# VectorE in program order for the last two expert units of layer 0, with the merge of read-back results moved

## The chip, the cores and the metric

The kernel is one program on one NeuronCore of a Trainium2 chip. A core has TensorE (PE, the matrix engine; PEld is its weight load), VectorE (DVE), ScalarE (ACT), GpSimd (POOL) and SyncE (SP, which here only issues transfers). The engines run independently and wait for one another through semaphores; each executes its own queue in order. Transfers go through 16 DMA engines. The metric is device microseconds of one execution; the median of three runs of the kernel before is 1012.01 us.

## The reference

The reference is a transformer backbone of two layers over 256 context and 256 latent tokens, width 1024. Each layer has a mixer (layer 0 a recurrent one, layer 1 attention) and a mixture of experts. This is the part that matters here, with `t` the 512 normalised tokens of layer 0:

```python
e_val, e_idx = lax.top_k(e_sel, TOP_K)            # two experts for each token
...
for e in range(N_EXPERTS):                        # 16 experts, hidden width 512
    he = jax.nn.silu(t @ w1[e]) * (t @ w3[e])
    out = out + comb[:, e:e + 1] * (he @ w2[e]).astype(F32)
...
xl = xl + g2l * hier_moe(hl2, ...)                # the residual, gated
```

Layer 1 begins with an RMS norm of that sum, and then the qkv projection.

## The kernel before, in words

The 16 experts of layer 0 are computed in 12 units (`NU`), each on at most 128 gathered rows. Units with `SEQ[e] >= BIG` serve two experts, 64 rows each, straight from the loaded weights (`raw`) in f32; the others split each weight half into a high and a low part (`whi` by ScalarE, `wlo` by VectorE) and take three matmuls for one product. In the loop over `e` from line 1825 a unit has these steps: first inner product (`hidden(e, 0, ...)`, issued one unit ahead), `sl` = silu of it, second inner product (`hidden(e, 1, 0)` and `hidden(e, 1, 1)`), `he` = product of both (line 1840), its transposes, `hh` and, for split units, the low part `hl` (line 1853), then the output product in two accumulators `py`. While unit `e` waits for `he`, the first inner product of unit `e + 1` is on PE.

The loop's last two units are positions 10 (split; `SEQ` 7) and 11 (two experts; `SEQ` 11). The results of positions 0 to 9 are scattered to a buffer `yd` in HBM. The results of the last two stay on chip: `yh` and `yl` are the high and low part of `py` times the routing weight, and `finish_moe` multiplies them by a one-hot matrix (`back`) to bring them back to token order.

At position 10 (`NU - N_LAST`) `get_parts` lets GpSimd read `yd` back: two transfers of 512 KB (`ya`, `yb`) for each of four tiles of 128 tokens, in the order `F_ORDER` = 2, 3, 0, 1. For tiles 0 and 1 both halves lie in a buffer named `pt`. `merge(t)` (line 1813) adds `ya` and `yb`, multiplies by the gate row and adds the sum to the residual `xres[t]`: four VectorE instructions, of which the multiplication is two. In `finish_moe` (line 1902) the products of the last two units are gated and added to `xres`; from it comes the norm of layer 1.

The order of instructions: without a pin a scheduler places an engine's instructions by priority and dependence as it estimates them. `pin(where)` reads the table `PIN` (line 61) and keeps the engines named there (p PE, a ScalarE, d VectorE, g GpSimd) in the order of the program text, until the next `pin`. `m0` before the loop pins PE alone; `fin` behind it has no entry, so nothing is pinned from there.

Weights come from one planned list by SyncE; a load is issued when its buffer comes free. Behind the weights of unit 11 (twelve loads of 1 MB, of which the last is the one called the twelfth) the list goes on with loads for layer 1 (`w_ada`, `w_qkv`). All computing instructions carry line 131 in the profile, since a helper issues them; they are told apart by tile names.

Of the kernel before, what the change touches and what calls it, by code (L numbers as in the profile page):

```python
# [27 lines left out]
NU = 12  # L28
# [29 lines left out]
N_ADA = 2  # L58
Q0 = (0, 0, 2, 2, 2, 2, 1, 1, 1, 1)
LT_ACT = 1  # L60
PIN = dict(pair='p', px='padg', re='da', tb='dag', m0='p', n1='pad', xa='pad')
AT_SUM = 1
N_SP0 = 2
N_OH = 1
# [38 lines left out]
F_ORDER = (2, 3, 0, 1)  # L103
# [35 lines left out]
def backbone(ctx, tc, I, out):  # L139
# [3 lines left out]
    def pin(where):  # L143
        names = PIN.get(where, "")
        for e, nm in ((act, "a"), (dve, "d"), (pool, "g"), (pe, "p"), (sp, "s")):
            e.on = nm in names
# [11 lines left out]
    def acc():  # L158
        return acc_p.tile([P, 512], F32, tag="acc", name="acc")

    def aux():
        return aux_p.tile([P, 512], F32, tag="aux", name="aux")
# [68 lines left out]
    def feed(key):  # L231
        state["fed"] = where[key]
        pump(state["fed"] + len(slots))
        return loaded.pop(key)

    def less_slots(pl):
        state["turn"] = sum(p is not pl for p, _ in slots[:state["turn"]])
        slots[:] = [x for x in slots if x[0] is not pl]
# [306 lines left out]
    def high_if(x):  # L545
        return tc.high_priority() if x else ExitStack()

    def mm3(ps, a, b, first, last):

        pe.matmul(ps, a[0], b[0], start=first, stop=False)  # L550
        pe.matmul(ps, a[0], b[1], start=False, stop=False)
        pe.matmul(ps, a[1], b[0], start=False, stop=last)
# [219 lines left out]
    def fetch_moe(l, d4, t, NT):  # L772
        ys = d4("ya"), d4("yb")
        for k, y in enumerate(ys):
            (sp if l else pool).dma_start(y, yd[l][(k * NT + t) * P:(k * NT + t + 1) * P, :])
        return ys
# [483 lines left out]
    def wide(name="w"):  # L1260
        if name in IN_B.split():
            return raw2_p.tile([P, 2048], F32, tag="raw", name=name).rearrange("p (m n) -> p m n", m=4)
        return wp.tile([P, 4, 512], F32, tag="w", name=name)
# [34 lines left out]
    xa, u = wide("xa"), wide("u")  # L1298
# [149 lines left out]
    for d in range(2):  # L1448
        seq = list(range(8)) if d == 0 else [3, 2, 1, 0, 7, 6, 5, 4]
        for ct in range(2):  # L1450
            n4 = 2 * d + ct
            dsb = [aux(), aux()]
            for c in seq[:-1]:
                pr, t = c % 2, c // 2
# [39 lines left out]
    for tpr in range(2):  # L1494
# [29 lines left out]
        for ti in range(2):  # L1524
            t = 2 * tpr + ti
# [123 lines left out]
    def d4(name):  # L1649
        return wk.tile([P, D], F32, tag="d4", name=name, bufs=N_D4)  # L1650
# [9 lines left out]
    def fetch_x(i):  # L1660
        if i < NU:
            if i < 2:
                xg = xgs[i] = xg01[:, i * D:(i + 1) * D]
            else:
                xg = xgs[i] = d4("xg")
            if 2 <= i < N_D4:
                pool.memset(xg, 0.0)
            gather(0, xg, ix[:, SEQ[i]:SEQ[i] + 1])
# [41 lines left out]
    def halves(ps, lhsT, raws, sl, first, last):  # L1710

        for o in range(2):
            c = slice(o * (P // 2), (o + 1) * (P // 2))
            pe.matmul(ps[c, :], lhsT[:, c], raws[o][:, sl], start=first, stop=last)
# [15 lines left out]
    def quarters(i, n, h):  # L1730
        ahead()
        for q in range(2):
            yield q, *split_of.pop(((i, n, h), q))
            state["done"] += 1
            ahead()

    def hidden(i, n, h):
        if h == 0:
            hs[i, n] = acc()
        xh, xl = xs[i]  # L1740
        if SEQ[i] >= BIG:
            raws = [feed((n, 0, i, o, h)) for o in range(2)]
            for kk in range(4):
                k = 4 * h + kk
                halves(hs[i, n], xh[:, k, :], raws, slice(kk * 512, (kk + 1) * 512), k == 0, k == KD - 1)
            return
        for q, wh, wl in quarters(i, n, h):
            for kk in range(2):
                k = 4 * h + 2 * q + kk
                mm3(hs[i, n], (xh[:, k, :], xl[:, k, :]), [x[:, kk * 512:(kk + 1) * 512] for x in (wh, wl)],  # L1750
                    k == 0, k == KD - 1)
# [51 lines left out]
    def get_parts():  # L1803

        state["cap"] = len(order)
        for t in F_ORDER:
            if t < N_PARTS:
                pt = parts_p.tile([P, 2048], F32, tag="raw", name="pt")
                parts[t] = fetch_moe(0, {"ya": pt[:, 0:D], "yb": pt[:, D:2 * D]}.get, t, 4)
            else:  # L1810
                parts[t] = fetch_moe(0, d4, t, 4)

    def merge(t):

        ya, yb = parts[t]
        dve.tensor_tensor(ya, ya, yb, op=ALU.add)
        for n in range(2):
            sl = slice(n * 512, (n + 1) * 512)
            dve.tensor_tensor(ya[:, sl], ya[:, sl], g2[int(t < 2)][n], op=ALU.mult)
        dve.tensor_tensor(xres[:, t, :], xres[:, t, :], ya, op=ALU.add)  # L1820
# [4 lines left out]
    for e in range(NU):  # L1825
        two = SEQ[e] >= BIG
        if AHEAD > 2:
            fetch_x(e + AHEAD)
        if e == NU - N_LAST:
            get_parts()  # L1830
        sl = wk.tile([P, 512], F32, tag="sl", name="sl")
        act.activation(sl, hs[e, 0], AF.Silu)
        hidden(e, 1, 0)
        if e == NU - 1:
            for t in F_ORDER[:2]:
                merge(t)
        hidden(e, 1, 1)
        he = wk.tile([P, 4, P], F32, tag="he", name="he")
        with high_if(HE):
            dve.tensor_tensor(he.rearrange("q k p -> q p k"), sl.rearrange("q (p k) -> q p k", k=4),  # L1840
                              hs[e, 1].rearrange("q (p k) -> q p k", k=4), op=ALU.mult)
        if e + 1 < NU:
            hidden(e + 1, 0, 0)
        ps = aux()
        for k in range(4):
            pe.transpose(ps[:, k * P:(k + 1) * P], he[:, k, :], ident)
        hh = wk.tile([P, 512], F32 if two else F32R, tag="hh", name="hf" if two else "hh")
        if not two:
            hl = wk.tile([P, 512], F32R, tag="hl", name="hl")
        with high_if(HE):  # L1850
            act.activation(hh, ps, AF.Copy)
            if not two:
                dve.tensor_tensor(hl, ps, hh.bitcast(F32), op=ALU.subtract)
        if e + 1 < NU:
            hidden(e + 1, 0, 1)
        if e == NU - 1:
            for t in F_ORDER[2:]:
                merge(t)
        py = [acc(), acc()]
        for h in range(2):  # L1860
            if two:
                raws = [feed((2, 0, e, o, h)) for o in range(2)]
                for n in range(2):
                    for kk in range(2):
                        k = 2 * h + kk
                        halves(py[n], hh[:, k * P:(k + 1) * P], raws,
                               slice(kk * D + n * 512, kk * D + (n + 1) * 512), k == 0, k == 3)
            else:
                for q, wh, wl in quarters(e, 2, h):
                    k = 2 * h + q  # L1870
                    ks = slice(k * P, (k + 1) * P)
                    for n in range(2):
                        ws = slice(n * 512, (n + 1) * 512)
                        mm3(py[n], (hh[:, ks], hl[:, ks]), (wh[:, ws], wl[:, ws]), k == 0, k == 3)
            if h == 0 and e + 2 < NU:
                prep_x(e + 2)
        if e == NU - LESS:
            less_slots(parts_p)
        if e == 1:
            last_ow = d4("ow")  # L1880
            for n in range(N_LAST):
                last_tokens(NU - 1 - n)
            A1B1 = ada_cols(1)
        if e == 2:
            for n in range(N_LAST):
                turn_last(NU - 1 - n)
        if e == 4:
            g2 = [rows_pe(rowt, i, 2, mod[0], 2) for i in range(2)]
        if e >= NU - N_LAST:
            yh, yl = last_y[e] = [wk.tile([P, D], F32R, tag="d4", name="yl", bufs=N_D4) for _ in range(2)]  # L1890
            for n in range(2):
                sl = slice(n * 512, (n + 1) * 512)
                act.activation(yh[:, sl], py[n], AF.Copy, scale=wgt[:, SEQ[e]:SEQ[e] + 1])
                dve.scalar_tensor_tensor(yl[:, sl], py[n], wgt[:, SEQ[e]:SEQ[e] + 1], yh[:, sl].bitcast(F32),
                                         op0=ALU.mult, op1=ALU.subtract)
        else:
            y = d4("y")
            for n in range(2):
                act.activation(y[:, n * 512:(n + 1) * 512], py[n], AF.Copy, scale=wgt[:, SEQ[e]:SEQ[e] + 1])
            scatter(0, ix[:, NU + SEQ[e]:NU + SEQ[e] + 1], y)  # L1900
# [76 lines left out]
    px = ExitStack()  # L1977
# [533 lines left out]
```

## Time and profile before

| | |
|---|---|
| timed runs | 1014.98, 1012.01, 1007.88 us (median 1012.01) |
| the profiled execution | 1008.28 us, its span 1006.6 us |
| PE busy | 905.5 us (90% of the span) |
| VectorE busy | 540.6 us (54%) |
| ScalarE busy | 396.5 us (39%) |
| GpSimd busy | 130.3 us (13%) |
| read from HBM | 294.76 MB |
| memory rate over the span | 305 GB/s |

The profile is one execution. In the timeline a row is: start and duration in us, engine, line, operation, written tile `<-` read tiles, count of instructions merged in the row, and in brackets the idle time of the engine before it and what ended that. Matmuls are pipelined, so a row's duration is longer than the step from one start to the next. In the queue's tables q1 holds SyncE's transfers and q0 GpSimd's.

### The profile page before, as it was taken

Reading aid. Unit: us, or ns where it says so; the run is one execution under the profiler, and the core shown is the slowest. Engines: PE = TensorE matmul, PEld = TensorE weight load, DVE = VectorE, ACT = ScalarE, POOL = GpSimd, SP = SyncE. Lnnn points to the kernel's source line nnn. Section 1 sums busy time; section 2 is a strip of 40 time slices with the busy share of each in tenths; the row PEclk is TensorE's granted clock in tenths of the full one; section 3 lists DMA queues with packets and bytes.
Section 4 is the critical chain, followed back from the end, with each engine's and each line's share of the span. In section 5 each row is a group of like instructions: output and inputs, shape, how many; then the busy total and the mean of one; then the engine's idle time right before and its main releaser. Section 6 shows DMA issues by size and latency. Waiting matters only on the chain. (4 is left out here: it accounts for less than half of the span.)

```text
span 1006.6 us, 12582 instructions
## 1 busy us (share of the span) xinstructions
PE 905.5 (90%) x4565; PEld 535.6 (53%) x4565; DVE 540.6 (54%) x1040; ACT 396.5 (39%) x686; POOL 130.3 (13%) x142
## 2 busy tenths in 40 slices
PE   5999989999964989999999377999996999999997
PEld 3556456667744647457568133764574444443442
DVE  5495777458684656428468357787656111111112
ACT  3465472234322637347468104543644221121210
POOL 1011520133302112100001100133001000000000
PEclk9999999999995999999999788999998899999999
DMA  9957353488453899999998957655758699999994
GB/s 311 385 177 271 126 209 124 170 299 299 147 185 137 309 418 419 419 420 411 415 420 347 402 211 291 257 208 211 271 200 334 231 416 418 415 417 414 417 413 159
DMA packets 63166, 304.56 MB, mean 303 GB/s; under 512 B 8579, under 2 KB 17667, under 8 KB 35057
## 3 DMA queue, kind: packets, MB, share of 16 engines
q1 hardware_dynamic: 55216, 284.56, 72.5%
q0 software_dynamic: 5120, 14.06, 3.6%
q10 hardware_dynamic: 2752, 4.98, 1.3%
q8 instruction: 40, 0.66, 0.3%
q14 instruction: 38, 0.30, 0.1%
HBM read 294.76 MB, written 12.58 MB: 305 GB/s over the span
## 5 line engine op out<-in xcount | busy, mean ns | idle before, releaser
L131 DVE TENSOR_TENSOR wlo<-raw,whi 128x1024 fp32r<-128x1024 f32 x144 | 174.3, 1231 | 64.7 <-ACT whi L131 62.4
L131 ACT ACTIVATE whi<-raw 128x1024 fp32r<-128x1024 f32 x140 | 145.6, 1057 | 99.5 <-PE acc L131 86.3
L131 PE MATMUL aux<-raw,x 128*64 128x512 f32 x488 | 116.3, 597 | 1.1 <-ACT x L131 0.7
L131 PEld LDWEIGHTS aux<-raw,x 128*64 128x64 f32 x488 | 34.4, 137 | 62.3 <-issue 58.4
L131 PE MATMUL acc<-raw,xf 128*64 128x512 f32 x256 | 61.9, 598 | 2.9 <-DMA raw<-in_w_dram 2.9
L131 PE MATMUL aux<-raw,sl 128*64 128x512 f32 x240 | 57.0, 594 | 0.7 <-ACT sl L131 0.7
L131 PE MATMUL ada<-raw,cT 128*32 128x512 f32 x320 | 56.4, 613 | 0.1
L131 PE MATMUL acc<-whi,xh 128*128 128x512 f32 x128 | 51.9, 405 | 0.0
L131 PE MATMUL acc<-wlo,xh 128*128 128x512 f32 x128 | 50.1, 391 | 0.8 <-DVE wlo L131 0.8
L131 PE MATMUL acc<-whi,xl 128*128 128x512 f32 x128 | 50.1, 391 | 0.0
L131 PE MATMUL acc<-whi,hl 128*128 128x512 f32 x64 | 26.4, 413 | 20.5 <-DVE hl L131 20.5
L131 DVE SCALAR_TENSOR_TENSOR aux<-aux,ws,mod 128x512 f32<-128x512 f32 x8 | 6.1, 758 | 71.6 <-PE aux L131 71.6
L131 PE MATMUL acc<-whi,h 128*128 128x512 f32 x128 | 43.1, 410 | 0.0
L131 PE MATMUL acc<-hhi,whi 128*128 128x512 f32 x96 | 37.0, 415 | 3.3 <-ACT hhi L131 2.8
L131 PEld LDWEIGHTS acc<-raw,xf 128*64 128x64 f32 x256 | 19.2, 136 | 38.6 <-issue 30.0
L131 DVE TENSOR_TENSOR he<-sl,aux 128x512 f32<-128x512 f32 x8 | 8.5, 1057 | 56.2 <-PE aux L131 56.2
L131 PE MATMUL acc<-raw,hf 128*64 128x512 f32 x128 | 34.5, 600 | 4.3 <-DMA raw<-in_w_dram 4.3
L131 POOL DMA_INDIRECT yd<-y,ix x10 | 11.9, 1192 | 198.5 <-ACT y L131 182.2
L131 PEld LDWEIGHTS aux<-raw,sl 128*64 128x64 f32 x240 | 17.8, 137 | 35.8 <-issue 33.7
L131 PE MATMUL acc<-hlo,whi 128*128 128x512 f32 x96 | 35.9, 409 | 0.0
L131 PE MATMUL acc<-hhi,wlo 128*128 128x512 f32 x96 | 35.0, 400 | 0.0
L131 ACT ACTIVATE x<-gat,B,A 128x256 f32<-128x256 f32 x26 | 13.3, 561 | 41.6 <-PE gat L131 40.8
(438 smaller groups left out, 1823.9 us busy)
## 6 DMA issues: line engine op xcount, KB each, us to landing
raw<-in_w_dram SPq DMA_DIRECT2D x151, 1024.0 KB, 15.0
raw<-in_w_ada_dram SPq DMA_DIRECT2D x38, 1024.0 KB, 5.4
raw<-in_w_dram SPq DMA_DIRECT2D x72, 512.0 KB, 12.1
raw<-in_w_in_dram SPq DMA_DIRECT2D x10, 1024.0 KB, 6.0
raw<-in_w_ada_dram SPq DMA_DIRECT2D x32, 256.0 KB, 7.6
raw<-in_w_qkv_dram SPq DMA_DIRECT2D x6, 1024.0 KB, 7.2
xres<-in_w_dram SPq DMA_DIRECT2D x5, 1024.0 KB, 8.4
raw<-in_w_out_dram SPq DMA_DIRECT2D x4, 1024.0 KB, 7.4
```

Source lines behind the costliest of these rows:

```text
L131: ins = f(*a, **k)
```

## The change

`PIN` gets an entry `m1` for PE and VectorE, taken at position 10, so that from there to `fin` VectorE too is kept in the order of the text. The merges of tiles 2 and 3, which stood inside unit 11's second inner product, go behind that product and its `he`, where the merges of tiles 0 and 1 already stood.

```diff
-PIN = dict(pair='p', px='padg', re='da', tb='dag', m0='p', n1='pad', xa='pad')
+PIN = dict(pair='p', px='padg', re='da', tb='dag', m0='p', m1='pd', n1='pad', xa='pad')
@@
         if e == NU - N_LAST:
+            pin("m1")
             get_parts()
         sl = wk.tile([P, 512], F32, tag="sl", name="sl")
         act.activation(sl, hs[e, 0], AF.Silu)
         hidden(e, 1, 0)
-        if e == NU - 1:
-            for t in F_ORDER[:2]:
-                merge(t)
         hidden(e, 1, 1)
@@
         if e + 1 < NU:
             hidden(e + 1, 0, 1)
         if e == NU - 1:
-            for t in F_ORDER[2:]:
+            for t in F_ORDER:
                 merge(t)
```

VectorE's queue around `he` and `hl` of unit 10, before (numbers are buffer numbers; ya_5278 and yb_5279 are tile 2's read-backs, ya_5282 tile 3's, acc_5294 is unit 10's second inner product):

```order
L131 TENSOR_TENSOR wlo_5314<-raw_5048,whi_5313 128x1024
L131 TENSOR_TENSOR he_5339<-sl_5292,acc_5294 128x128x4
L131 TENSOR_TENSOR wlo_5326<-raw_5086,whi_5325 128x1024
L131 TENSOR_TENSOR wlo_5336<-raw_5086,whi_5335 128x1024
L131 TENSOR_TENSOR ya_5278<-ya_5278,yb_5279 128x1024
L131 TENSOR_TENSOR ya_5278<-ya_5278,row_4441 128x512
L131 TENSOR_TENSOR ya_5278<-ya_5278,row_4445 128x512
L131 TENSOR_TENSOR xres_104<-xres_104,ya_5278 128x1024
L131 TENSOR_TENSOR ya_5282<-ya_5282,yb_5283 128x1024
L131 TENSOR_TENSOR ya_5282<-ya_5282,row_4441 128x512
L131 TENSOR_TENSOR hl_5360<-aux_5354,hh_5359 128x512
L131 TENSOR_TENSOR ya_5282<-ya_5282,row_4445 128x512
```

The same place in VectorE's queue of the changed kernel (he_5434 is unit 11's, yl_5402 unit 10's):

```order
L131 TENSOR_TENSOR wlo_5314<-raw_5048,whi_5313 128x1024
L131 TENSOR_TENSOR wlo_5326<-raw_5086,whi_5325 128x1024
L131 TENSOR_TENSOR wlo_5336<-raw_5086,whi_5335 128x1024
L131 TENSOR_TENSOR he_5339<-sl_5292,acc_5294 128x128x4
L131 TENSOR_TENSOR hl_5360<-aux_5354,hh_5359 128x512
L131 SCALAR_TENSOR_TENSOR yl_5402<-acc_5375,wgt_2576,yl_5401 128x512
L131 SCALAR_TENSOR_TENSOR yl_5402<-acc_5376,wgt_2576,yl_5401 128x512
L131 TENSOR_TENSOR he_5434<-sl_5407,acc_5409 128x128x4
L131 TENSOR_TENSOR ya_5278<-ya_5278,yb_5279 128x1024
```

`hl` stood behind six merge instructions and stands now ahead of all of them; `he` of unit 10 went behind two `wlo`; and `he` of unit 11 went ahead of the merges.

VectorE's queue around `yl` of unit 11, before (pt_5286 and pt_5289 are tiles 0 and 1; acc_5459 and acc_5460 are unit 11's output, acc_5491 the first product of `finish_moe`):

```order
L131 TENSOR_TENSOR xres_104<-xres_104,pt_5289 128x1024
L131 SCALAR_TENSOR_TENSOR yl_5402<-acc_5375,wgt_2576,yl_5401 128x512
L131 SCALAR_TENSOR_TENSOR yl_5402<-acc_5376,wgt_2576,yl_5401 128x512
L131 TENSOR_TENSOR he_5442<-sl_5407,acc_5409 128x128x4
L131 SCALAR_TENSOR_TENSOR yl_5486<-acc_5459,wgt_2576,yl_5485 128x512
L131 TENSOR_TENSOR pt_5286<-acc_5491,row_4449 128x512
L131 SCALAR_TENSOR_TENSOR yl_5486<-acc_5460,wgt_2576,yl_5485 128x512
L131 TENSOR_TENSOR xres_104<-xres_104,pt_5286 128x512
```

And in the changed kernel:

```order
L131 TENSOR_TENSOR pt_5289<-pt_5289 128x1024
L131 TENSOR_TENSOR pt_5289<-pt_5289,row_4449 128x512
L131 TENSOR_TENSOR pt_5289<-pt_5289,row_4453 128x512
L131 TENSOR_TENSOR xres_104<-xres_104,pt_5289 128x1024
L131 SCALAR_TENSOR_TENSOR yl_5486<-acc_5459,wgt_2576,yl_5485 128x512
L131 SCALAR_TENSOR_TENSOR yl_5486<-acc_5460,wgt_2576,yl_5485 128x512
L131 TENSOR_TENSOR pt_5286<-acc_5491,row_4449 128x512
L131 TENSOR_TENSOR pt_5286<-aux_5501,row_4453 128x512
```

All four merges now stand directly ahead of unit 11's `yl`, and both `yl` ahead of the first finishing instruction. PE's queue is the same up to `finish_moe`, SyncE's throughout; in `finish_moe` PE's products are interleaved a little differently with the adaLN products (`ada`).

## Rows read from the trace of the kernel before

**Rows 1.** Waits of PE, 560 to 640 us (tile <- releaser: us, times, longest)

```profile
PE acc L131 <- DVE hl L131: 20.5, 1, 20.5
```

**Rows 2.** Timeline of PE around the long wait

```profile
558.01 0.66 PE L131 MATMUL aux<-ident,he 128*128 128x128 f32 x4
...
562.52 0.40 PE L131 MATMUL acc<-wlo,hh 128*128 128x512 f32 x1
583.41 0.80 PE L131 MATMUL acc<-whi,hl 128*128 128x512 f32 x1 [20.50 <-DVE hl L131]
...
587.85 0.47 PE L131 MATMUL acc<-whi,hh 128*128 128x512 f32 x1
...
589.79 0.39 PE L131 MATMUL acc<-whi,hl 128*128 128x512 f32 x1
```

**Rows 3.** Timeline of DVE, 550 to 600 us

```profile
554.78 1.07 DVE L131 TENSOR_TENSOR he<-sl,acc 128x512 f32<-128x512 f32 x1
555.69 2.34 DVE L131 TENSOR_TENSOR wlo<-raw,whi 128x1024 fp32r<-128x1024 f32 x2
573.43 1.23 DVE L131 TENSOR_TENSOR ya<-ya,yb 128x1024 f32<-128x1024 f32 x1 [15.40 <-issue]
...
576.01 1.23 DVE L131 TENSOR_TENSOR xres<-xres,ya 128x1024 f32<-128x1024 f32 x1
580.80 1.23 DVE L131 TENSOR_TENSOR ya<-ya,yb 128x1024 f32<-128x1024 f32 x1 [3.56 <-DMA yb<-yd]
...
582.67 0.68 DVE L131 TENSOR_TENSOR hl<-aux,hh 128x512 fp32r<-128x512 f32 x1
```

**Rows 4.** DMA queues, 566 to 576 us (packets, MB, share of 16 engines)

```profile
q1 hardware_dynamic: 376, 2.76, 65.9%
q0 software_dynamic: 381, 1.43, 35.2%
```

**Rows 5.** DMA queues, 576 to 586 us

```profile
q0 software_dynamic: 743, 2.65, 66.2%
q1 hardware_dynamic: 82, 0.52, 12.7%
```

**Rows 6.** Timeline of PE behind the wait, unit 11's products

```profile
590.82 7.09 PE L131 MATMUL acc<-raw,xf 128*64 128x512 f32 x32
...
600.58 3.65 PE L131 MATMUL acc<-raw,hf 128*64 128x512 f32 x16
...
606.50 3.65 PE L131 MATMUL acc<-raw,hf 128*64 128x512 f32 x14
```

**Rows 7.** Issues of SP's queue: unit 11's last three loads

```profile
562.27 0.91 SPq L131 DMA_DIRECT2D raw<-in_w_dram  x2
594.50 0.33 SPq L131 DMA_DIRECT2D raw<-in_w_dram  x1
```

**Rows 8.** DMA issues, 562.8 to 564 us (KB each, median us to landing)

```profile
raw<-in_w_dram SPq DMA_DIRECT2D x1, 1024.0 KB, 18.3
```

**Rows 9.** The tile pt, 540 to 640 us: its transfers

```profile
L131 POOL DMA_DIRECT2D pt<-yd x4: 537/538/538, 563.7 to 565.3; - x4
...
DMA to landing us min/median/max: 19.4/20.1/20.8
```

**Rows 10.** Timeline of DVE, 590 to 680 us

```profile
610.86 0.69 DVE L131 TENSOR_TENSOR pt<-acc,row 128x512 f32<-128x512 f32 x1 [0.92 <-PE acc L131]
611.47 0.74 DVE L131 SCALAR_TENSOR_TENSOR yl<-acc,wgt,yl 128x512 fp32r<-128x512 f32 x1
```

**Rows 11.** Stretches: PE, PEld, DVE, ACT, POOL, PEclk, DMA, GB/s

```profile
565.00:570.00 5.00, 0.00 (x0) 0.00 (x0) 0.00 (x0) 0.00 (x0) 0.80 (x2) 0.75 1.02 425
...
585.00:590.00 5.00, 5.00 (x17) 3.95 (x16) 5.00 (x7) 0.00 (x0) 0.00 (x0) 0.70 0.01 6
590.00:595.00 5.00, 5.00 (x24) 1.87 (x24) 3.45 (x5) 1.38 (x2) 0.00 (x0) 1.00 0.01 3
```

**Rows 12.** The page: busy tenths of the DMA engines in 40 slices

```profile
DMA  9957353488453899999998957655758699999994
```

## Prediction

> **What bounds the kernel now.** I began with the waits of TensorE (PE). Between 560 and 640 us PE has one long wait, 20.5 us for the VectorE (DVE) tile hl [rows 1]. The PE timeline gives the place: after two matmuls of the second layer of the last-but-one expert unit (loop position 10), PE stands from 562.9 to 583.4 [rows 2]. The DVE timeline gives the cause: hl is computed at 582.67, although PE began the transposes for its input at 558.01 [rows 2]. In front of it in DVE's queue stand the merge instructions of token tiles 2 and 3; the first starts at 573.43 and the second tile's at 580.80, and the latter row names the read-back transfer `yb<-yd` as what it waited for [rows 3]. So an instruction that PE needs is queued behind work that needs late transfers, and no arithmetic is short.
>
> Then I read what the transfers do meanwhile. From 566 to 576 two queues are at work: q1, SyncE's weights, moves 2.76 MB, and q0, GpSimd's read-backs, 1.43 MB [rows 4]; from 576 on q0 moves its last 2.65 MB and q1 only 0.52 MB [rows 5]. q1 dries up because its next weight half (the twelfth of unit 11) has no free buffer: it is issued at 594.50, when PE, 32 us after the one before, has used up the first pair of that unit's second inner product [rows 6, 7]. This is the point that decides the size of the gain.
>
> **The change part by part.** No instruction is added or removed on any engine. The pin puts DVE in program order for units 10 and 11, and the merges come behind he of unit 11. PE and SyncE keep their order around this place.
>
> *he of unit 10 behind two wlo.* Before, he starts at 554.78, and two wlo follow in 2.34 us; now they go first, so he ends at about 558.2. PE turns to its transposes at 558.01 [rows 2, 3]. Loss 0 to 0.2 us, and none of it reaches the end, since hl (0.68 us) is due only at 562.9 and needs only the transposes and the copy hh behind them, which PE and ScalarE do at once.
>
> *hl before the merges.* hl is then ready near 560.3, and PE runs on at 562.9. 22 of the 24 matmuls of that layer are left, at 0.243 us each (eight from 587.85 to 589.79): end at 568.2. Before, ten of them ran from 583.41 to 587.85 at 0.444 us [rows 2]. Next come the 32 matmuls of unit 11's second inner product, 7.09 us, to 575.3; then he, transposes and copy, which took 2.67 us before (597.91 to 600.58), to 578.0; and 16 matmuls of 3.65 us to 581.6 [rows 6]. The weights for these were issued by 563.2 and the last of them landed 18.3 us after its issue, at 581.1 [rows 7, 8]; the earlier ones landed before, so they don't stop PE. The twelfth half now goes out at 571.9, when its buffer comes free. 1.05 MB at q1's rate beside q0, 0.276 MB/us [rows 4], is 3.8 us: landed at 584.9, if it follows the one before it. PE's last 16 matmuls end at 588.5. Before, they ended at 610.1. Were PE the only thing, 21.6 us would be won.
>
> *The merges and yl of unit 11.* Now the new wait. DVE's order is he of unit 11 (done about 576.4), four merges, then the two yl of unit 11, and behind these everything that finishes the layer. What is queued behind a waiting merge is thus yl, and PE waits for yl with its products by the one-hot matrix, and so does the next layer. A merge takes 3.8 us (573.43 to 577.24 [rows 3]). Tiles 2 and 3 have their data at 573.4 and 580.8. Tiles 0 and 1 (named pt) are the last four transfers of q0: issued to 565.3, landing at most 20.8 us later, at 586.1 [rows 9]. That is the landing of before, with q1 dry. Now q1 isn't dry. It holds the twelfth half and an ada load from 571.9, two qkv loads from 575.3, two more from 581.6 and two from 588.5: 8.9 MB from 576 on with the 0.52 MB still owed. So q0 doesn't get the engines alone.
>
> Bounds for the last read-back: 586.1, if it lands as before; and if q1 always went first, 8.9 MB at 0.419 MB/us (both queues together, 566 to 576) and then 2.65 MB, that is 576 + 21.2 + 6.3 = 603.5. I take the share seen while both had work, because that is exactly the state that now goes on: 2.65 MB / 0.143 MB/us = 18.5 us, so 594.5 [rows 4, 5]. In packets the two queues then are level, 376 to 381 [rows 4], and the weights' packets are twice as large.
>
> The Trainium skill (DMA: Bandwidth & Descriptors, Issuing engines are not separate DMA queues) says that transfers issued by different engines run on the same 16 DMA engines and interleave. By it weights that set out sooner are taken from the read-backs' rate, which speaks against the change; the level packet counts agree with it. By a private path for GpSimd's reads the sum would be 6.5 us better.
>
> *The sum.* Last merge 594.5 to 598.3, two yl at 0.7 us: 599.7. Before, the second yl ended at 611.47 + 0.74 = 612.2 [rows 10], so 12.5 us are won there. Two things come off. Before, one finishing product (610.86 [rows 10]) ran ahead of the second yl and now comes behind: 0.7 us. And PE idles from 588.5 to 599.7; in the old stall its granted clock fell below full, 0.75 from 565 to 570 [rows 11], so the first products for yl run at 1.2 GHz, two of them in the path at some 0.2 us more: 0.4 us. **Gain 11.4 us.**
>
> *Does it reach the end?* From 612 on a chain of DVE and ScalarE (xres, square sums, pt<-xres) sets the pace, and its transfers were issued earlier. Behind slice 22 (the stall) the DMA engines are full again only in slices 32 to 38, counted from 0, the last expert stage [rows 12], which starts when the layer's routing and free buffers let it and so moves with the chain. I pass on the whole of it.
>
> Its own execution of 1008.28 us (span 1006.6) becomes 996.9. The median shown, 1012.01, would become 1000.6. The profiled execution lies near the fastest of the timed ones (1007.88 to 1014.98), so I forecast nearer the median: **1000 us**.
>
> **The rivals.**
> 1. *The read-backs land as before* (586.1). Then the merges run back to back from 576.4 and 580.8 to 592.2, yl to 593.6: 612.2 - 593.6 - 0.7 = 17.9 us, 994 us. For it: DVE's second merge waited only to 580.8 and q0 finished in 5.3 us after that. Against: it finished so fast with q1 empty [rows 5].
> 2. *The read-backs give way to weights.* At the other bound (603.5) the merge ends at 607.3, yl at 608.7: 3.5 us less 1.1, so 2.4 us, about 1010 us. The same would show if a later stage soaked up the gain. For it: q1 gets two thirds of the bytes already. Against: q0's 0.143 MB/us never sank while both worked.
> 3. *Slower: TensorE's clock.* A matmul at 1.2 GHz costs 0.20 us more (0.444 to 0.243 [rows 2]). If after the new idle stretch the clock stayed at the lower level through the finishing and the dense qkv stage, 57 matmuls eat the 11.4 us, and 107 make it 1% slower, 1022 us. For it: the finishing is full of small PE gaps. Against: after the old stall the clock rose within ten matmuls, 0.70 in 585 to 590 and 1.00 right after [rows 11].
> 4. *The pin doesn't free hl.* 1012 us. Excluded by the new order, where hl stands ahead of all merges: no chance given.
>
> **How the numbers follow.** Forecast 0.55, rival 1 0.22, rival 2 0.19, rival 3 0.04. A change of 1%, 10 us, is about what timing this kernel can tell from none. The forecast of 11.4 us lies just over that; I count six tenths of its chance as over, since three runs of before spread over 7 us. With all of rival 1 that is 0.55 faster, 0.41 within 1%, 0.04 slower. The range runs from 992 (rival 1, with a run as good as the profiled one) to 1007 (the near half of rival 2). The forecast's own range, two microseconds of doubt about the last landing and three about the median, is 995 to 1005.
>
> **What would show it.** PE's wait for hl is gone, and PE's last weights matmul of unit 11 ends near 588. The merge of tile 1 starts near 594.5, after a DVE wait named as a read-back; pt lands some 29 us after its issue, not 20. The second yl ends near 600, and PE shows a wait of about 11 us for yl. In 576 to 586 q1 moves over 2.5 MB, not 0.52. A landing at 586 means rival 1; one past 600, rival 2; long stretches of clock 0.5 after 600, rival 3. The forecast would be wrong if q0's share changed with what q1 carries, or if a weight half stopped PE earlier than 581.

## The result, and the profile after

| | before | after |
|---|---|---|
| median | 1012.01 us | 999.61 us (998.3 to 1005.76, five executions) |
| ratio | | 0.9898, 95% interval 0.9858 to 0.9937 |
| profiled execution (span) | 1008.28 us (1006.6) | 1005.76 us (1004.1) |
| TensorE busy | 905.5 us | 908.9 us |

A repeat beside a fresh set of the kernel before (e9 below) gave 1004.31 against 1012.22 us, ratio 0.9905 (0.9877 to 0.9933). The change gains about 1%: by these ratios 10.3 and 9.6 us, where 12 us lie between the medians of the first row.

The two profiled spans differ by only 2.5 us, so they can't be laid on one another from their starts. In the profile after, PE's transposes of unit 10's `he` come at 561.92 us and in that of before at 558.01 [rows 2], though the code ahead of them has not changed. I therefore measure everything from these transposes and call them the anchor; a time of after less 3.9 us is a time in the clock of before. (Whether that is right is what e12 looks at.) As the far end of the stretch I take "kv", the first kv matmul of layer 1 (`acc<-whi,h`): 69.3 us from the anchor before, 60.7 after. Before and after:

```profile
627.33 0.80 PE L131 MATMUL acc<-whi,h 128*128 128x512 f32 x1
```

```profile
622.66 0.80 PE L131 MATMUL acc<-whi,h 128*128 128x512 f32 x1
```

PE's waits after, 560 to 640 us (tile <- releaser: us, times, longest), in place of [rows 1]:

```profile
PE acc L131 <- DVE yl L131: 11.3, 1, 11.3
PE aux L131 <- DVE pt L131: 4.7, 2, 3.5
PE aux L131 <- DVE he L131: 1.2, 1, 1.2
PE acc L131 <- DMA raw<-in_w_dram: 1.0, 1, 1.0
```

The 20.5 us for hl are gone. In their place stands one wait of 11.3 us, for yl, and 1.0 us for a weight half. PE's timeline after, against [rows 2, 6]:

```profile
561.92 0.66 PE L131 MATMUL aux<-ident,he 128*128 128x128 f32 x4
...
571.56 0.39 PE L131 MATMUL acc<-whi,hl 128*128 128x512 f32 x1
571.88 7.09 PE L131 MATMUL acc<-raw,xf 128*64 128x512 f32 x32
...
588.68 3.65 PE L131 MATMUL acc<-raw,hf 128*64 128x512 f32 x14 [1.05 <-DMA raw<-in_w_dram]
...
606.93 2.07 PE L131 MATMUL acc<-yl,back 128*128 128x512 f32 x4 [11.31 <-DVE yl L131]
```

PE runs through unit 10's output product at full pace and ends unit 11's weights at 592.3 (588.4 in the clock of before, where it was 610.1). Then it stands. DVE's timeline shows for what, against [rows 3, 10]:

```profile
563.24 0.69 DVE L131 TENSOR_TENSOR hl<-aux,hh 128x512 fp32r<-128x512 f32 x1 [1.38 <-ACT hh L131]
...
579.04 1.03 DVE L131 TENSOR_TENSOR he<-sl,acc 128x512 f32<-128x512 f32 x1 [5.58 <-PE acc L131]
579.92 1.20 DVE L131 TENSOR_TENSOR ya<-ya,yb 128x1024 f32<-128x1024 f32 x1
...
587.35 1.22 DVE L131 TENSOR_TENSOR ya<-ya,yb 128x1024 f32<-128x1024 f32 x1 [3.64 <-DMA yb<-yd]
...
594.88 1.23 DVE L131 TENSOR_TENSOR pt<-pt 128x1024 f32<-128x1024 f32 x1 [3.73 <-DMA pt<-yd]
...
602.40 1.23 DVE L131 TENSOR_TENSOR pt<-pt 128x1024 f32<-128x1024 f32 x1 [3.70 <-DMA pt<-yd]
...
606.13 1.40 DVE L131 SCALAR_TENSOR_TENSOR yl<-acc,wgt,yl 128x512 fp32r<-128x512 f32 x2
```

The merges start 7.5 us apart and each but the first waits for a read-back by name; a merge itself takes 3.8 us. The yl of unit 11 stand behind the last. The transfers of tile pt, against [rows 9]:

```profile
L131 POOL DMA_DIRECT2D pt<-yd x4: 540/540/540, 568.0 to 569.6; - x4
...
DMA to landing us min/median/max: 29.5/31.1/32.7
```

The DMA queues after, 576 to 586 us (packets, MB, share of 16 engines), against [rows 5]:

```profile
q1 hardware_dynamic: 384, 2.83, 68.3%
q0 software_dynamic: 377, 1.35, 33.7%
```

Where q1 ran dry before (0.52 MB), it now moves 2.83 MB beside the read-backs; in the same stretch of the clock of before (579.9 to 589.9 here) it is 2.78 MB beside 1.36. The level number of packets (384 to 377; before, 376 to 381 in [rows 4]) agrees with what the Trainium skill (DMA: Bandwidth & Descriptors, Issuing engines are not separate DMA queues) says of transfers that share the 16 engines.

### The profile page after: what moved, and what is told of

The parts are those of the page before. It is cut to its first block, busy times and chain, and to the rows that moved or that the text cites. A ratio compares the mean times of both kernels' runs of the same rounds, so it can differ in the third digit from the quotient of the medians.

```text
span 1004.1 us, 12587 instructions
## 1 busy us (share of the span) xinstructions
PE 908.9 (91%) x4565; PEld 535.4 (53%) x4565; DVE 542.5 (54%) x1040; ACT 396.6 (39%) x686; POOL 131.6 (13%) x142
## 5 line engine op out<-in xcount | busy, mean ns | idle before, releaser
L131 PE MATMUL acc<-whi,hhi 128*128 128x512 f32 x64 | 27.5, 429 | 1.8 <-ACT v L131 1.8
```

What stands on the lines that cost most here:

```text
L131: ins = f(*a, **k)
```

## The experiments

The timed ones are compared with the kernel before on the same chip (medians 1011.3 to 1012.2 us); e7 and e12 are single executions, read for their traces. "Kv" is counted from the anchor.

**e1, the pin alone.** Before with `m1='pd'` taken at position 10; the merges of tiles 2 and 3 stay inside unit 11's second inner product.

```diff
-PIN = dict(..., m0='p', n1='pad', xa='pad')
+PIN = dict(..., m0='p', m1='pd', n1='pad', xa='pad')
...
         if e == NU - N_LAST:
+            pin("m1")
             get_parts()
```

> VectorE pinned as in the change, the merges of tiles 2 and 3 left inside unit 11's second inner product. Theory (the last read-back sets the end): hl is free, he of unit 11 waits for the merge of tile 3, so PE stands some 11 us before its transposes; but PE then ends its weights some 5 us before the last merge, which still waits for the last read-back. Time within 3 us of the changed kernel, 997 to 1003 us. Rival (PE's path sets the end, each part of the change is worth half): about 1006 us.

Measured: 1002.44 us, ratio 0.9911 (0.9881 to 0.9942); kv 59.2. PE's wait of this kernel:

```profile
PE aux L131 <- DVE he L131: 11.9, 1, 11.9
```

The time is the theory's. The pin alone gives the gain as far as it can be told: the interval overlaps those of the changed kernel, and kv is 59.2 against 60.7 and 59.4 (e9). That moving the merges adds anything to the pin is not shown. The wait merely sits one step earlier, at he of unit 11 behind two merges instead of at yl behind four. One part of the theory missed: PE ends its weights at 605.2, level with the last merge (604.9) and not 5 us ahead of it.

**e2, the move without the pin.** The changed kernel without the entry `m1`. `pin("m1")` is still called, and without an entry it pins nothing, so from position 10 PE too loses the pin that it has in both kernels (`m0`). The edit takes away more than DVE's order.

```diff
-PIN = dict(..., m0='p', m1='pd', n1='pad', xa='pad')
+PIN = dict(..., m0='p', n1='pad', xa='pad')
...
         if e == NU - N_LAST:
             pin("m1")
```

> Merges moved as in the change, VectorE not pinned: the scheduler then puts all four merges behind hl but ahead of yl of unit 10 and he of unit 11. Theory: he of unit 11 waits for the last read-back (near 592 to 598 us), and then come PE's transposes and 32 more matmuls, some 12 us; second yl near 612, as in the kernel before: 1007 to 1014 us. Rival (hl alone was the loss, so freeing it gives the gain whatever waits behind): 997 to 1003 us.

Measured: 1012.83 us, ratio 1.0018 (1.0001 to 1.0034); kv 72.8. PE's longest wait, and DVE's timeline where it ends:

```profile
PE aux L131 <- DVE he L131: 21.4, 2, 20.0
```

```profile
597.88 1.23 DVE L131 TENSOR_TENSOR pt<-pt 128x1024 f32<-128x1024 f32 x1 [4.43 <-DMA pt<-yd]
...
603.28 1.02 DVE L131 TENSOR_TENSOR he<-sl,acc 128x512 f32<-128x512 f32 x1
```

Without the pin hl comes early enough, but the scheduler puts all four merges ahead of unit 11's he, where the text has them behind it. The stall moves from hl to he and keeps its size. PE's order changed as well: before, the 32 matmuls of unit 11's first inner product stand half ahead of the anchor and half behind it, all ahead of unit 10's output product; here all stand behind the anchor, and 30 of them among the matmuls of that product. So the anchor lies earlier in PE's order, kv 72.8 can't be set beside the others, and the time is not that of DVE's order alone.

**e3, the competition taken away.** The changed kernel, but SyncE's ada load behind unit 11's weights, and with it all that follows on its queue, waits until the last read-back has landed: a one-column copy by GpSimd from the read-back into the load's buffer (`behind` names what must have landed, `from` the load of the list).

```diff
-                if state["behind"] is not None:
+                if state["behind"] is not None and state["next"] >= state.get("from", 0):
                     pool.tensor_copy(r[:, 0:1], state["behind"])
...
+        state["behind"] = parts[F_ORDER[-1]][1][:, 0:1]
+        state["from"] = where[2, 0, NU - 1, 1, 1] + 1
```

> The changed kernel, but SyncE's first load behind unit 11 (ada) waits until the last read-back has landed, by one GpSimd copy of one column from that tile into the load's buffer. Theory (the weights take two thirds of the rate from the read-backs): in the 10 us before its landing the last read-back has q0 at over 0.3 MB/us, pt lands some 22 us after its issue, not 31, PE's wait for yl falls from 11 to 2 to 4 us, and the time falls by 6 to 9 us, to 991 to 994 us. Rival 1 (q0 has a pace of its own of 0.14 MB/us): pt at 30 us, time not better, 999 to 1003. Rival 2 (the ada and qkv loads become late in their turn): pt lands early, but PE or ScalarE waits for raw, 997 to 1002.

Measured: 999.44 us, ratio 0.9893 (0.9862 to 0.9925); kv 55.7. Landing of pt, then SP's and PE's timelines:

```profile
DMA to landing us min/median/max: 21.1/22.3/23.4
```

```profile
594.29 0.34 SPq L131 DMA_DIRECT2D raw<-in_w_ada_dram  x1
```

```profile
599.27 1.89 PE L131 MATMUL ada<-raw,cT 128*32 128x512 f32 x2 [5.55 <-DMA raw<-in_w_ada_dram]
```

The last read-back lands 9 us sooner when the weights keep away, and the second yl ends 36.9 us from the anchor (45.6 in the changed kernel). So the competition is shown. The rate behind it was expected too high: in the 10 us before the landing q0 moved 0.23 MB/us and not over 0.3, since the twelfth half was still on its way. But PE's ada products stand ahead of its products for yl, and their load went out only at 594.29: PE waits 5.6 us there, and of the 8.7 us won at yl 5.0 arrive at kv. The time was not the theory's but that of rival 2.

**e4, the merges behind yl.** The changed kernel with the four merges placed behind unit 11's yl.

```diff
-            for t in F_ORDER:
-                merge(t)
...
             (yl of unit 11)
+            if e == NU - 1:
+                for t in F_ORDER:
+                    merge(t)
```

> The changed kernel with the four merges behind yl of unit 11. Theory: PE doesn't wait for yl any more, but what finishes tiles 0 and 1 needs their merges and so still the last read-back, landing as in the changed kernel, some 32 us after its issue. Only yl (1.4 us), PE's first products and the finishing of tiles 2 and 3 leave the path: 3 to 5 us better, 994 to 997 us. Rival (the wait for yl itself is the bound, the merges are not): its 11 us come back, 988 to 991 us.

Measured: 1007.83 us, ratio 0.9968 (0.9948 to 0.9988); kv 62.1. Both expectations were wrong. DVE's timeline:

```profile
594.64 0.75 DVE L131 SCALAR_TENSOR_TENSOR yl<-acc,wgt,yl 128x512 fp32r<-128x512 f32 x1 [0.97 <-ACT yl L131]
595.30 1.21 DVE L131 TENSOR_TENSOR ya<-ya,yb 128x1024 f32<-128x1024 f32 x1
...
610.35 1.21 DVE L131 TENSOR_TENSOR pt<-pt 128x1024 f32<-128x1024 f32 x1
```

yl no longer waits for a read-back, but 15 us of merging, in the changed kernel done while the next read-back was awaited, now stand behind yl and ahead of the norm that kv needs. The wait for read-backs was not idle time that could be had for nothing. Behind kv 1.7 us more are lost: the router of layer 1 (`pl<-xT,rw`) stands 201.1 us from the anchor, after 198.0.

**e5, only the qkv loads held.** As e3 from the next load on, so that the first ada load goes out unhindered.

```diff
-        state["from"] = where[2, 0, NU - 1, 1, 1] + 1
+        state["from"] = where[2, 0, NU - 1, 1, 1] + 2
```

> The changed kernel, but SyncE's loads from the first qkv load behind unit 11 on wait until the last read-back (pt) has landed; the first ada load, which made TensorE wait in e3_hold, goes out unhindered. Theory (the competition of these loads sets the landing of the last read-back and with it yl of unit 11; the ada load was what the hold of e3 gave back): pt lands some 24 to 26 us after its issue (32.7 in the changed kernel, 23.4 in e3), the second yl ends about 39 us behind the transposes of he of unit 10 (45.6 in the changed kernel, 36.9 in e3), TensorE's wait for ada is under 2 us, the first kv matmul comes about 54 us behind those transposes (60.7); 992 to 996 us, some 5 us under the changed kernel. Rival A (the qkv or the second ada load held back becomes the new wait): a wait of 4 us or more of TensorE for raw of w_qkv or w_ada, kv at 58 or later, 998 us or more. Rival B (locally won time doesn't reach the end): kv near 54, yet over 998 us.

Measured: 999.75 us, ratio 0.9885 (0.9864 to 0.9906); kv 54.3. PE's wait, and the landing of pt:

```profile
PE acc L131 <- DVE yl L131: 4.4, 1, 4.4
```

```profile
DMA to landing us min/median/max: 24.2/25.3/26.0
```

In the trace all came as the theory has it (kv 54, no wait for ada, the second yl at 39.1), and the profiled execution was 995.79 us. The median was not: rival B by the time, with what was won locally not in the median of five executions. I return to this at e12.

**e6 and e10, the hold ends with tile 0's read-back.** As e3, released one tile's read-back sooner; e10 is the same kernel again.

```diff
-        state["behind"] = parts[F_ORDER[-1]][1][:, 0:1]
+        state["behind"] = parts[F_ORDER[-2]][1][:, 0:1]
```

> As e3_hold, but the ada load and all behind it wait for the read-back of tile 0, which lands ahead of tile 1's. Theory: tile 0 lands some 22 us after its issue, the ada load goes out about 1.5 us sooner than in e3 and tile 1 lands some 2 us later than there (25 us after issue), since it now shares the engines with the ada load; TensorE's wait for ada shrinks from 5.6 to about 4 us; the first kv matmul about 55 us behind the transposes of he of unit 10, as in e3 within 1.5 us: 996 to 1000 us. Rival (the two tiles' packets alternate so that they land together): nothing changes against e3 by more than 0.5 us in the trace.

> e6_hold_t0 again, unchanged, beside the changed kernel on the same chip. Theory (its local gain of some 9 us up to the first kv matmul reaches the end): first kv matmul 52 us behind the transposes of he of unit 10 (51.8 in e6), 993 to 997 us, 4 to 6 us under the changed kernel of the same call. Rival (the 994.45 us of e6 were five lucky executions): 998 to 1000 us, level with the changed kernel.

Measured: 994.45 us, ratio 0.9828 (0.9802 to 0.9853), and again 997.67 us, 0.9854 (0.9831 to 0.9878); kv 51.8 and 54.4. PE's waits in e6, and its products for yl:

```profile
PE ada L131 <- DMA raw<-in_w_ada_dram: 4.7, 2, 2.9
```

```profile
601.70 1.20 PE L131 MATMUL acc<-yl,back 128*128 128x512 f32 x4
...
603.20 1.52 PE L131 MATMUL acc<-yl,back 128*128 128x512 f32 x6
```

The ada load went out 2.3 us sooner than in e3, counted from the anchor, and the last read-back landed no later (23.3 us after its issue), against my 25. Both expectations missed in part: e6 came out below its 996 to 1000 us (kv 51.8, not 55), e10 just above its 993 to 997 (kv 54.4, not 52), 6.6 us under the changed kernel on the same chip. In both the second yl ends 37 us from the anchor. What differs behind it is PE's ada products ahead of the products for yl, in e6 and in e10:

```profile
599.10 1.02 PE L131 MATMUL ada<-raw,cT 128*32 128x512 f32 x2 [2.93 <-DMA raw<-in_w_ada_dram]
```

```profile
595.68 1.89 PE L131 MATMUL ada<-raw,cT 128*32 128x512 f32 x2 [3.09 <-DMA raw<-in_w_ada_dram]
```

The waits are alike, but the granted clock is 1.00 from 600 to 605 in e6 and 0.50 from 595 to 600 in e10, where the products for yl start 2.4 us after the second yl and not at once. From the end of the wait to those products it is 2.6 us in e6 and 4.8 in e10, so most of the 2.5 us between the two kv goes with the clock.

That is the best kernel of this study: over both runs nine executions from 992.8 to 998.62 us, where the changed kernel has eleven from 998.3 to 1007.58. It beats both kernels.

**e7, no read-backs at all.**

```diff
-                parts[t] = fetch_moe(0, d4, t, 4)
+                parts[t] = d4("ya"), d4("yb")
+                for y in parts[t]:
+                    pool.memset(y, 0.0)
```

> The changed kernel without the eight read-backs (the tiles are set to zero, so that the merges run on zeros and the output is not the reference's; the routing of layer 1 changes, and only the stretch up to the kv products is read). Theory: with the data there, the four merges run back to back behind he of unit 11 (4 times 3.8 us, 15.2 us), so the second yl ends about 34 us behind the transposes of he of unit 10 (45.6 in the changed kernel, 54 before); TensorE waits under 4 us for yl (11.3), and no more than 2 us for the twelfth weight half, which now lands sooner. The first kv matmul comes about 49 us behind the transposes (60.7). Rival (the twelfth weight half or the ada load holds TensorE, not the read-backs): yl ends at 40 us or later, or TensorE's wait for raw grows over 4 us.

PE's wait for yl, and DVE's yl:

```profile
PE acc L131 <- DVE yl L131: 1.1, 1, 1.1
```

```profile
596.52 1.40 DVE L131 SCALAR_TENSOR_TENSOR yl<-acc,wgt,yl 128x512 fp32r<-128x512 f32 x2
```

The second yl ends 34.3 us from the anchor and kv comes at 48.3: the theory's 34 and 49. Nothing but the landing of the read-backs, and the 15.2 us of merging behind he, holds yl.

**e8, only tiles 0 and 1 merged ahead of yl**, read back first; tiles 2 and 3 are merged ahead of their own finishing, DVE in program order there too.

```diff
-PIN = dict(..., n1='pad', xa='pad')
+PIN = dict(..., n1='pad', xa='pad', fin='d')
-F_ORDER = (2, 3, 0, 1)
+F_ORDER = (0, 1, 2, 3)
-            for t in F_ORDER:
+            for t in F_ORDER[:2]:
                 merge(t)
...
+    for t in F_ORDER[2:]:
+        merge(t)
     finish_moe(2)
```

> The changed kernel with the read-backs in the order 0, 1, 2, 3 and only tiles 0 and 1 merged ahead of yl of unit 11; tiles 2 and 3 are merged ahead of their own finishing, with VectorE in program order there too. Theory (yl waits for the last read-back that is merged ahead of it): yl no longer waits for the last four transfers; the merge ahead of it waits for tile 1, the second in the queue, which lands near 587 instead of 598.4 in the clock of before, so the second yl ends near 35 us behind the transposes of he of unit 10 (45.6); TensorE's wait for yl falls from 11.3 to under 3 us. 7.5 us of merging then come behind the finishing of tiles 0 and 1, and their read-backs land near 600: 995 to 1000 us. Rival (the merges that now stand behind yl give it back, as in e4_yl_first): 1001 to 1006 us, with VectorE busy without gaps from yl to the last norm of the four tiles.

Measured: 1008.77 us, ratio 0.9968 (0.9953 to 0.9983); kv 49.3. Yl ended 32.5 us from the anchor and PE did not wait for it, as the theory has it, and kv came 11 us sooner than after; all of it and more was then lost, to over the rival's bound. DVE and PE later on:

```profile
623.69 1.22 DVE L131 TENSOR_TENSOR ya<-ya,yb 128x1024 f32<-128x1024 f32 x1
```

```profile
634.20 1.94 PE L131 MATMUL ada<-raw,cT 128*32 128x512 f32 x8 [4.10 <-DMA raw<-in_w_ada_dram]
641.44 0.87 PE L131 MATMUL aux<-ident,xn 128*128 128x128 f32 x3 [5.30 <-DVE xn L131]
```

Tile 2's merge ran only at 623.69, behind all the kv arithmetic of the first two tiles, and PE waited for the norm of tiles 2 and 3 and for the ada load. At the router the kernel stands 201 us from the anchor. The run changes the place of two merges and the pin of the finishing together, so how much each of them lost is not shown.

**e9 and e11**: the changed kernel again, and the cures of e5 and e6 together.

> The changed kernel again, unchanged, for two things: timed on the same chip beside the next two, and a second profile of it. Theory (the profiled execution of the changed kernel came 3.9 us late to this place by a lower granted clock of TensorE at its start, which is not the change's): in the new profile the first kv matmul again comes about 60.7 us behind the transposes of he of unit 10 (within 1 us), the last read-back again lands 31 to 33.5 us after its issue, and the transposes themselves lie anywhere from 557 to 565 us: 998 to 1002 us. Rival (the change moves the part ahead of unit 10): the transposes lie at 561.9 within 0.5 us again, with the granted clock of 0 to 50 us at 0.90 again.

> Both cures together: SyncE's loads wait from the first qkv load on (as e5), and only for tile 0's last read-back (as e6). Theory: the ada load is unhindered (wait of TensorE for ada under 2 us) and the last read-back lands as in e5, 24 to 27 us after its issue; the first kv matmul 53 to 55 us behind the transposes of he of unit 10: 995 to 998 us, not better than e6, since what the free ada load saves it costs in the landing. Rival (the two savings add): kv at 51 or earlier, 990 to 994 us.

Measured: e9 1004.31 us, anchor at 564.86, kv 59.4, and

```profile
DMA to landing us min/median/max: 22.3/27.1/32.0
```

So e9's landing is the expected one, but its time lies above the 998 to 1002 us and its kv 1.3 us below the expected 60.7; the granted clock of the first 50 us is 0.90 as in the first profile, though the anchor is 2.9 us later, so the theory that this clock made the first profile late is not borne out. e11 999.86 us, ratio 0.9864 (0.9839 to 0.9889), kv 54.1: in the trace as expected, no better than e6, and the time 2 us above.

**e12, the kernel before again.**

> The kernel before again, unchanged, for a second profile of it, since all distances in this study are taken from the transposes of he of unit 10. Theory (the stretch ahead of unit 10 varies from execution to execution by some microseconds, and the first profile of the kernel before, of 1008.28 us where the median is 1012, was an early one): the transposes of he of unit 10 lie between 558 and 565 us, later than 558.0; the wait for hl is 20.5 us within 0.5, the first kv matmul comes 69.3 us behind the transposes within 1.5 us, and pt lands at most 20.8 us after its issue within 1 us. Rival (the changed kernels are slower ahead of unit 10): the transposes lie at 558.0 within 0.5 us again although the whole execution is 1010 us or more.

Measured: 1014.11 us. PE's timeline, and the stretch of 0 to 50 us (PE, PEld, DVE, ACT, POOL, PEclk, DMA, GB/s) here and in the changed kernel:

```profile
563.74 0.66 PE L131 MATMUL aux<-ident,he 128*128 128x128 f32 x4
...
589.38 0.79 PE L131 MATMUL acc<-whi,hl 128*128 128x512 f32 x1 [20.73 <-DVE hl L131]
```

```profile
0.00:50.00 50.00, 37.29 (x175) 22.10 (x176) 23.50 (x76) 16.07 (x27) 2.68 (x12) 0.86 0.98 347
```

```profile
0.00:50.00 50.00, 37.79 (x183) 22.89 (x184) 23.53 (x76) 17.52 (x28) 2.69 (x12) 0.90 0.98 347
```

The anchor of the same kernel moved by 5.7 us, while from it everything stood as before: 20.7 us for hl, kv 69.5, and 448.7 us from the anchor to the span's end (448.6 in the first profile). So the anchor is the right zero, the first profile of before was an early one, and some 5 us of difference between two executions arise ahead of unit 10. In the other twelve profiles that have the anchor at this place in PE's order (all but e2) it lies between 558.5 and 564.9. Kv from the anchor still differs between two profiles of one kernel, by 0.1 us (before), 1.4 (the changed kernel) and 2.5 (e6 and e10), so smaller differences of kv say little.

A median of few executions moves with the anchor: the two of the changed kernel are 999.61 and 1004.31 us. For e5 the trace adds that from the anchor to the span's end it took 435.6 us, where the changed kernel took 442.2 and 438.7 (e9): in that execution what was won locally does reach the end. Why its median does not show it stays open.

## Why the prediction was right

999.61 us against 1000 predicted, in the range; the repeat's 1004.31 lies in it too. By the ratios the gain is 1.02%, and 0.95% in the repeat, so on which side of the 1% of the chances it came out was luck. The mechanism was the forecast's. Step by step, in the clock of before:

- *hl before the merges:* PE's last weights matmul ended at 588.4 (588.5 predicted), with a wait of 1.0 us for the twelfth half. Right. He behind two wlo cost nothing seen.
- *The merges and yl:* the new wait stands where it was put. That it lasts 11.3 us (11 predicted) is in part luck: PE first ran 3.4 us of products that the working left out (by the one-hot matrix, and ada), so it stands from 591.7 to 603.0, not from 588.5 to 599.7, and the late landing made up for that. The read-backs compete with SyncE's loads at 0.135 to 0.141 MB/us (0.143 assumed); e3 and e7 show that this is what sets yl.
- *The last landing* is the term that was mis-sized. The merge of tile 1 starts at 598.5, not 594.5; pt lands 32.7 us after its issue (32.0 in e9), not 29. About 1.6 us of the difference are rate and bytes: from 579.9 (576 in the clock of before) q0 still moves 2.78 MB at 0.138 MB/us, where I had 2.65 at 0.143. The rest, 2.3 us, is the end of the queue, for which the working had no term: the division by a rate treats the last packet like the others. The queue q0 after, 600 to 601 and 601 to 602 us (packets, MB, share):

```profile
q0 software_dynamic: 12, 0.02, 5.4%
```

```profile
q0 software_dynamic: 2, 0.00, 1.1%
```

  The megabytes are through by 600, the last two packets come between 601 and 602, and DVE is let go at 602.4. Why the last packets come so late no run shows.
- *The two deductions* (0.7 for a finishing product, 0.4 for PE's cold clock) are not seen: from the second yl to kv it is 15.1 us before, after and in e9. PE's clock was as low as forecast (0.50 from 607 to 610), but that did not reach kv. So the gain is 8.6 us at yl and 8.6 at kv; in e9 10.0 and 9.9. Forecast: 11.4.
- *Does it reach the end?* Yes in e9: 438.7 us from the anchor to the end against 448.6, so 9.9. In the first profile of after only 6.4; at the router it was still 7.9. The 1.5 us between are lost in the last expert unit, where its 32 products took 8.81 us and in before 7.11 (the chain that ended last, after and before):

```profile
987.36 8.81 PE aux L131 x32
```

```profile
991.60 7.11 PE aux L131 x32
```

  From 988 to 991 the granted clock was 0.52 in after and 1.00 in e9. After and e9, 980 to 990 us:

```profile
980.00:990.00 10.00, 8.04 (x36) 2.55 (x34) 1.03 (x1) 0.60 (x1) 0.00 (x0) 0.87 0.50 199
```

```profile
980.00:990.00 10.00, 8.05 (x42) 2.67 (x40) 1.02 (x1) 0.60 (x1) 0.00 (x0) 1.00 0.61 243
```

- *The median:* taking the gain from the median shown rather than from the profiled execution was right; e12 shows that this one began 5.7 us earlier than another of the same kernel.

Of the rivals, the landing as before (rival 1) would have needed q1 empty; e3 and e6, which take part of q1's loads away, come nearest to it (23.4 and 23.3 us after issue against 20.8). The landing at 598.5 lies nearly half of the way to rival 2. The clock (rival 3) did not stay low: 0.74 from 611.9 to 631.9, about where it was 0.85 before, and 1.00 from there on. Rival 4 did not come: the wait for hl is gone. e2 shows a relative of it, the same stall at he, where neither DVE nor PE is pinned.

The level of the time owes something to luck: with the landing where it was, the working would have given 7.4 us, and the ratios give 9.6 and 10.3.

## What to carry to other kernels

An instruction that waits for a late transfer blocks all that stands behind it on its engine. Look for what the other engines need soonest among that, put it ahead, and ask at once what is then behind the same wait. A stall also holds back the loads of other queues: when it goes, these loads start sooner and take bandwidth from the transfer that was waited for, so the gain is not the stall but what is left after this. Holding such loads back until the read-backs were nearly in (e6, e10) gave 5 to 7 us more here by the ratios. But a load that is held back can become the next wait: in e3 PE waited 5.6 us for one, and the time was no better than that of the changed kernel's first set.

## What the runs showed of the hardware

- Where two queues had work they moved nearly equal numbers of packets, so bytes in the ratio of their packet sizes: 384 to 377 packets, 2.83 to 1.35 MB in 10 us (before, 376 to 381 and 2.76 to 1.43 MB).
- After an idle stretch PE's first products can be slow well past the first few: ten products for yl took 4.7 us after the 11.3 us wait (2.07 and 2.64; granted clock 0.53 from 606.9 to 612.3), and 2.7 us (1.20 and 1.52) in e6, at clock 1.00. Waits of equal length need not be followed by the same clock: behind 2.9 us in e6 it was 1.00, behind 3.1 us in e10, the same kernel, 0.50.
- The granted clock of the first 50 us differs from execution to execution of one kernel (0.97 and 0.86 in two profiles of before), and unit 10 lies at 558.0 and 563.7 us in them. That clock is not the only cause: in the two profiles of the changed kernel it is 0.90 both times, and unit 10 lies at 561.9 and 564.9; in e4 and e8 it is 0.97, and unit 10 lies at 562.9 and 562.7. What else moves it stays open.
